# Seven adaLN blocks moved off TensorE: products on GpSimd, sums on ScalarE

## The chip, the cores and the metric

One core of a Trainium2 chip runs the whole program. The metric is device time in microseconds (us): the median of several executions. TensorE multiplies matrices, VectorE and ScalarE do elementwise work, GpSimd does elementwise work and issues DMAs, and SyncE issues most DMAs. Each engine works through its own list of instructions in a fixed order; semaphores let one engine wait for another.

## The reference

Two layers of a diffusion trunk for 128 context tokens and 256 sample tokens, D = 2048, all in float32. In each layer, for both token groups g (context with c_ctx, sample with c):

```
m = silu(cond) @ w_mod + b_mod            # 2048 -> 6144: shift, scale, gate
h = rms_norm(x, g) * (1 + scale) + shift
x = x + gate * mixer(h)                   # mixer: h @ w_in, branches, @ w_out
```

Layer 0's mixer has a convolution of 31 taps with a layer norm on one branch, and attention with normalized q and k on the other. Layer 1's has windowed attention and a gated convolution of three taps. A final RMS norm gives the outputs. What the change touches is the first line, `silu(cond) @ w_mod`: a product of two vectors with a 2048 x 6144 matrix, twelve blocks of 512 output columns per layer.

## The kernel before

**Tokens and weights.** All 384 tokens are held at once, x transposed by features (`xT`, 128 partitions x 16 chunks x 384). Each float32 product is made of three faster ones: a weight tile `raw` of 128x1024 is split by ScalarE into a rounded part `whi` (L261) and by VectorE into the rest `wlo` (L262), and h likewise into `hhi` and `hlo`. A unit of weights by features (`feat_unit`, L354) is two such tiles, with 24 matmuls of 384 columns for each. So TensorE needs, for every 24 matmuls, one cast of ScalarE and one subtraction of VectorE. Weight tiles come on SyncE's queue through `NRAW` = 7 buffers.

**adaLN.** Three ways are used. (1) `mod_part` with `gemv_block` (L139): the vectors c_ctx and c, after SiLU, are 32 columns of stationary weights and the 512-column blocks of w_mod stream through TensorE, 16 matmuls for a block; four transposes (L172) bring the result from rows to partitions; `mod_finish` adds the bias. (2) `mod_vector` (L197): VectorE multiplies and adds, loads on GpSimd's queue; used for layer 1's shift and gate. (3) Layer 0's scale and shift, needed first, are made by way (1) at the start.

**Stages.** At the start come the q projection with layer 0's scale (`q_unit`, L571) and the key/value projection with its shift (L333). Then follow layer 0's projections by features: the convolution's inputs for four pairs of chunks, with 31 taps for each of 8 chunks on VectorE (`conv_steps`, L659, 240 steps of 399 columns) and attention (`attention0`) after the second pair; the layer norm (`ln_mean`, `ln_center`, `ln_out`), whose sums run on GpSimd (L702, L704, L718); and two groups of gate projections (L735, L528). Then the output projection adds to `xT` with `mods[0, 2]` as the gate (L543), and near its end `make_h(1, k)` needs `mods[1, 1]`. Layer 1 and the final norm follow.

**What sets the order.** A scheduler places instructions by priority. Background adaLN steps wait in `gemv_q`; after each unit of weights `pump` takes `bg["rate"]` of them. In layer 0 the queue holds the bias of q (`bias_q`, 8 steps), layer 0's gate (4 blocks) and three of the four blocks of layer 1's scale, 4 steps for each block. Taps and `mod_vector` steps are put `LATER` and fill VectorE's gaps. Each engine then runs its list in order.

Of the kernel before, what the change touches and what calls it, by code (L numbers as in the profile page):

```python
# [19 lines left out]
P = 128  # L20
# [18 lines left out]
NRAW = 7  # L39
# [3 lines left out]
R0 = 1.7  # L43
# [8 lines left out]
def trunk(ctx: ExitStack, tc: tile.TileContext, d: dict, o: dict):  # L52
# [128 lines left out]

    def mod_vector(layer, part, j, av, ring):
# [60 lines left out]
    xT = big.tile([P, KC, T], F32, tag="bigA", name="xT")  # L243

    def square_sum():
        av = tmp.tile([P, T], F32, tag="sacc", name="sacc", bufs=1)

        def each(f):
            if f == 0:
                nc.scalar.activation(av, xT[:, f, :], AF.Square)  # L250
            else:
                s = tmp.tile([P, T], F32, tag="wk", bufs=4, name="sqf")
                nc.scalar.activation(s, xT[:, f, :], AF.Square)  # L253
                nc.gpsimd.tensor_tensor(av, av, s, ALU.add)  # L254
        return av, each
# [8 lines left out]
    def make_h(layer, k):  # L264
        for g, c0, c1 in GROUPS:
            a = mods[layer, 1][:, k, g:g + 1]
            nc.scalar.activation(hhi[:, k, c0:c1], xT[:, k, c0:c1], AF.Copy, scale=a)  # L267
            nc.vector.scalar_tensor_tensor(hlo[:, k, c0:c1], xT[:, k, c0:c1], a, hhi[:, k, c0:c1].bitcast(F32),
                                           ALU.mult, ALU.subtract)

    def scale_norm(layer, dst, k, rb):
        for g, c0, c1 in GROUPS:
            ins = nc.vector.scalar_tensor_tensor(dst[:, c0:c1], xT[:, k, c0:c1], mods[layer, 1][:, k, g:g + 1],
                                                 rb[:, c0:c1], ALU.mult, ALU.mult).ins
            tc.add_manual_dep(ins, order["split"].name, NOSYNC, reason="weights first")
# [258 lines left out]
    def out_proj(layer, w, mix, units, each, split_last=0, between=None):  # L534
# [4 lines left out]
        def ev(fb):  # L539
            def go(j, ps):  # L540
                f = 2 * fb + j
                for g, c0, c1 in GROUPS:
                    nc.vector.scalar_tensor_tensor(xT[:, f, c0:c1], ps[:, c0:c1], gate[:, f, g:g + 1], xT[:, f, c0:c1],  # L543
                                                   ALU.mult, ALU.add)
                each(f)
            return go
# [32 lines left out]
    for j, nf in enumerate(widths):  # L579
        n = nf // P  # L580
        with first():
            for _ in range(2048 // (2048 // nf * P)):
                scale_q.pop(0)()
            sync_load(xT[:, k0:k0 + n, :], d["xT"][:, k0:k0 + n, :])
            for k in range(k0, k0 + n):
                make_h(0, k)
# [13 lines left out]
    load_tables()  # L600
    kT, v = qkv_state(0)
# [65 lines left out]
    gemv_q.extend(bias_q + mod_part(0, 2) + mod_part(1, 1, (512,) * 3))  # L667
# [63 lines left out]
    for fb in range(4):  # L731
# [4 lines left out]
        proj_feat(w0[8 + fb], ev_a)  # L736
    evb = gate_mul(mix, 8)
# [121 lines left out]
    def y_block(q, t, new=aux, after=True):  # L859
        py = new("y_ps")  # L860
        for i in range(4):
            ins = nc.tensor.transpose(py[:, i * P:(i + 1) * P], xT[:, 4 * q + i, t * P:(t + 1) * P], ident).ins  # L862
# [4 lines left out]
    def each(f):  # L867
# [4 lines left out]
        else:  # L872
            tail.append(tmp.tile([P, T], F32, tag="wk", bufs=4, name="sqf"))
            nc.scalar.activation(tail[-1], xT[:, f, :], AF.Square)
        nc.vector.tensor_scalar(xT[:, f, :], xT[:, f, :], vcol("final_norm_g", f), None, ALU.mult)
# [45 lines left out]
def _layout(inputs):  # L921
    a = {name: np.asarray(x) for name, x in inputs.items()}
    out = {name: a[name] for name in _AS_IS}
    out["vecs"] = np.concatenate([a[name].reshape(n, P).T for name, n in _VECS], axis=1)
    out["xT"] = _by_rows(np.concatenate([a["x_prompt"][0], a["x_sample"][0]]))
# [48 lines left out]
```

## Time and profile before

| | us |
|---|---|
| median of 3 runs (1297.65 to 1298.38) | 1298.0 |
| span of the profiled execution (the time that the profile has for it) | 1295.9 |
| TensorE busy, share of the span | 1267.4, 98% |
| VectorE busy, share | 882.0, 68% |
| ScalarE busy, share | 544.5, 42% |
| GpSimd busy, share | 142.2, 11% |

The profile shows one execution. Its page has the busy time of each engine, the same in 40 slices of the span, the chain of work that ended last, and groups of instructions by source line. Further views cut the span into windows, list one engine's groups or instructions in a window, and follow the chain there. In them PE is TensorE, DVE is VectorE, ACT is ScalarE, POOL is GpSimd and SP is SyncE. The durations of neighbouring instructions can overlap, above all on PE; the time that one adds is read from a run of them.

### The profile page before, as it was taken

The numbers are of one execution on the slowest core, as the hardware profiler recorded it, in microseconds if no ns is written. First come the engines' busy times: TensorE is split into PE (matmuls) and PEld (weight loads), VectorE is DVE, ScalarE is ACT, GpSimd is POOL, SyncE is SP. The second block draws the span as 40 slices with busy tenths as digits, with TensorE's granted clock in tenths as the row PEclk, the third lists the DMA queues.
The fourth block names the chain that finished last, engine by engine and source line by source line (L and its number), as shares of the span: only waits on it lengthen the run. The fifth ranks groups of instructions, "written<-read, shape, count | busy, mean of one in ns | idle before, by whom it ended". The sixth has DMA issues, their size and how long they took to land.

```text
span 1295.9 us, 18150 instructions
## 1 busy us (share of the span) xinstructions
PE 1267.4 (98%) x7000; PEld 1123.1 (87%) x7000; DVE 882.0 (68%) x1464; ACT 544.5 (42%) x941; POOL 142.2 (11%) x162
## 2 busy tenths in 40 slices
PE   6999999999999999999999999999999999999997
PEld 4566687888887888999999988899999999999997
DVE  2245627899999979989976932454544689996443
ACT  3344433644556645432363633344444422343332
POOL 0210100210000042122220000000000011111110
PEclk9999999999999999999999999999999999999998
DMA  9988867688654566676644444433333577764412
GB/s 364 403 309 313 300 185 258 232 307 295 226 166 160 196 221 218 209 225 217 199 135 130 121 128 130 123 118 109 98 99 103 185 231 229 252 194 146 123 50 98
DMA packets 71222, 252.76 MB, mean 195 GB/s; under 512 B 7456, under 2 KB 11808, under 8 KB 67552
## 3 DMA queue, kind: packets, MB, share of 16 engines
q1 hardware_dynamic: 59920, 211.90, 48.9%
q0 software_dynamic: 11072, 39.60, 9.8%
q8 instruction: 55, 0.90, 0.3%
q14 instruction: 31, 0.25, 0.1%
q10 hardware_dynamic: 144, 0.10, 0.0%
HBM read 247.91 MB, written 3.67 MB: 194 GB/s over the span
## 4 chain that ended last, share of the span: by engine, by line
PE 85%; DMA 5%; DVE 5%; issue 3%; POOL 1%; ACT 1%; SPq 0%; DVEq 0%; POOLq 0%; ACTq 0%
PE pf L354 57%; PE pt L333 10%; PE q L571 6%; PE gv L139 5%; DMA area<-in_mod_w 3%; DVE area L197 2%; PE s_ps L470 2%; PE o_ps L495 2%; DVE wlo L262 1%; DMA raw<-in_wf 1%; PE pT_ps L491 1%; DMA ring<-in_mod_w 1%; PE gv L172 1%; POOL lvar L718 1%; PE y_ps L862 1%
## 5 line engine op out<-in xcount | busy, mean ns | idle before, releaser
L354 PE MATMUL pf<-hhi,whi 128*128 128x384 f32 (+1 forms) x1664 | 569.2, 342 | 0.7 <-ACT whi L261 0.7
L354 PE MATMUL pf<-hlo,whi 128*128 128x384 f32 (+1 forms) x1664 | 569.7, 342 | 0.0
L354 PE MATMUL pf<-hhi,wlo 128*128 128x384 f32 (+1 forms) x1664 | 567.2, 343 | 1.7 <-DVE wlo L262 1.7
L262 DVE TENSOR_TENSOR wlo<-raw,whi 128x1024 fp32r<-128x1024 f32 x256 | 314.8, 1230 | 294.3 <-ACT whi L261 288.9
L261 ACT CAST whi<-raw 128x1024 fp32r<-128x1024 f32 x256 | 268.3, 1049 | 466.3 <-PE pf L354 242.5
L354 PEld LDWEIGHTS pf<-hhi,whi 128*128 128x128 f32 x1664 | 313.1, 188 | 24.0 <-issue 14.2
L354 PEld LDWEIGHTS pf<-hhi,wlo 128*128 128x128 f32 x1664 | 313.3, 188 | 9.8 <-issue 3.2
L354 PEld LDWEIGHTS pf<-hlo,whi 128*128 128x128 f32 x1664 | 313.6, 188 | 5.3 <-issue 2.9
L197 DVE SCALAR_TENSOR_TENSOR area<-area,cst 128x512 f32<-128x512 f32 x240 | 177.8, 777 | 14.7 <-DMA area<-in_mod_w 14.5
L659 DVE SCALAR_TENSOR_TENSOR cv<-apad,cw,cv 128x399 f32<-128x399 f32 x240 | 140.6, 635 | 1.1 <-ACT cv L657 0.8
L91 POOL DMA_DIRECT2D area<-in_mod_w x64 | 34.7, 542 | 424.0 <-DVE area L197 222.0
L333 PE MATMUL pt<-wlo,hhi 128*128 128x512 f32 x192 | 75.8, 395 | 0.0
L254 POOL TENSOR_TENSOR sacc<-sacc,sqf 128x384 f32<-128x384 f32 x43 | 55.2, 1284 | 186.9 <-ACT sqf L253 185.1
L333 PE MATMUL pt<-whi,hhi 128*128 128x512 f32 x192 | 75.7, 397 | 0.0
L333 PE MATMUL pt<-whi,hlo 128*128 128x512 f32 x192 | 75.0, 396 | 0.0
L333 PEld LDWEIGHTS pt<-whi,hhi 128*128 128x128 f32 x192 | 36.0, 188 | 12.4 <-ACT hhi L280 2.5
L571 PE MATMUL q<-whi,hhi 128*128 128x512 f32 x96 | 41.1, 428 | 4.4 <-ACT hhi L267 4.4
L478 ACT ACTIVATE pr<-s_ps,nm 128x384 f32<-128x384 f32 (+1 forms) x48 | 24.4, 509 | 49.7 <-DVE nm L477 34.7
L333 PEld LDWEIGHTS pt<-whi,hlo 128*128 128x128 f32 x192 | 36.0, 188 | 10.1 <-issue 0.8
L333 PEld LDWEIGHTS pt<-wlo,hhi 128*128 128x128 f32 x192 | 36.1, 188 | 9.0 <-issue 0.8
L139 PE MATMUL gv<-ring,cst 128*32 128x512 f32 (+1 forms) x288 | 35.8, 582 | 8.2 <-DMA ring<-in_mod_w 7.6
L571 PE MATMUL q<-wlo,hhi 128*128 128x512 f32 x96 | 40.5, 422 | 0.0
(171 smaller groups left out, 991.8 us busy)
## 6 DMA issues: line engine op xcount, KB each, us to landing
raw<-in_wf SPq DMA_DIRECT2D x144, 512.0 KB, 4.5
ring<-in_mod_w SPq DMA_DIRECT2D x32, 1024.0 KB, 7.5
area<-in_mod_w POOLq DMA_DIRECT2D x64, 512.0 KB, 4.6
raw<-in_w_out SPq DMA_DIRECT2D x64, 512.0 KB, 4.4
raw<-in_mod_w SPq DMA_DIRECT2D x56, 512.0 KB, 5.6
raw<-in_wq SPq DMA_DIRECT2D x32, 512.0 KB, 8.8
raw<-in_wt SPq DMA_DIRECT2D x24, 512.0 KB, 3.6
raw<-in_wkv SPq DMA_DIRECT2D x8, 512.0 KB, 7.8
```

What stands on the lines that cost most here:

```text
L91: ins = nc.gpsimd.dma_start(dst, src).ins
L139: nc.tensor.matmul(ps[32 * g:32 * g + 32, :nf], lhsT=stat(k), rhs=raw[:, i % raw.shape[1], :], start=(k < 4), stop=(k >= KC - 4))
L197: nc.vector.scalar_tensor_tensor(av[:, g], raw[:, i], cst[:, 2 * k + g:2 * k + g + 1], av[:, g], ALU.mult, ALU.add)
L254: nc.gpsimd.tensor_tensor(av, av, s, ALU.add)
L261: nc.scalar.copy(dst_hi, src)
L262: order["split"] = nc.vector.tensor_tensor(dst_lo, src, dst_hi.bitcast(F32), ALU.subtract).ins
L333: nc.tensor.matmul(pp[t], lhsT=x[:, k, tt], rhs=y[:, i, :], start=(k == 0 and n == 0), stop=(k == KC - 1 and n == 2))
L354: ins = nc.tensor.matmul(pp[j][:, :n], lhsT=x[:, i, fj], rhs=y[:, k, :n], start=(begin and k % 8 == 0 and m == 0), stop=(end and k % 8 == ...
L470: nc.tensor.matmul(ps, lhsT=mix[:, h0 + h, t * P:(t + 1) * P], rhs=kT[:, kv, c0:c0 + nk * P], start=True, stop=True)
L495: nc.tensor.matmul(po, lhsT=v[:, slots[j], kv * HD:(kv + 1) * HD], rhs=pT[:, j, :], start=(j == 0), stop=(j == nk - 1))
L571: nc.tensor.matmul(pq[b][t], lhsT=x[:, k, tt], rhs=y[:, 0, 512 * b:512 * b + 512], start=(k == 0 and n == 0), stop=(k == KC - 1 and n == 2))
L659: nc.vector.scalar_tensor_tensor(st["o"], apad[:, c, j:j + CVW], cw[:, c, j:j + 1], st["o"], ALU.mult, ALU.add)
```

## The change

The seven blocks that `gemv_q` held in layer 0 beside `bias_q` (layer 0's gate, four blocks, and three blocks of layer 1's scale) no longer go through TensorE. The weights of adaLN are laid out transposed in HBM as well (`modT`): a tile of 128x2048 has 128 output features as partitions and the 2048 inputs as columns. `load_crow` broadcasts c_ctx and c to all partitions and applies SiLU (`crow`, 128 x 2 x 2048). `mod_rows` then loads, for each block, four such tiles of 1 MB on GpSimd's queue; for each half tile and each of the two vectors GpSimd multiplies 1024 columns with `crow`, and ScalarE copies the product and accumulates its sum into `sm`. Seven blocks make 28 tiles, 112 products and 112 sums. `mod_finish` adds the two halves and the bias on VectorE.

The tiles and products take the room of `xT` (the tag bigA): after the key/value projection x is given up there, and after the last `done` it is loaded a second time, 3 MB on GpSimd's queue, as `xT2`, for the output projection. So `xT` becomes `x["T"]` all over the code. Further, `NRAW` falls from 7 to 6, `R0`, the rate of background steps at the start of layer 0, rises from 1.7 to 2.0, and the scratch for DMA descriptors is set to 2048.

```diff
-NRAW = 7
+NRAW = 6
-R0 = 1.7
+R0 = 2.0
...
+    crow = const.tile([P, 2, D], F32, name="crow")
+
+    def load_crow():
+        for g, name in enumerate(("c_ctx", "c")):
+            side_load(crow[:, g, :], d[f"row_{name}"].rearrange("(a f) -> a f", a=1).broadcast_to([P, D]))
+        for g in range(2):
+            nc.scalar.activation(crow[:, g, :], crow[:, g, :], AF.Silu)
+
+    def mod_rows(layer, part, j, slots):
+
+        if (layer, part) not in mods:
+            mod_tile(layer, part)
+        raws, prods = slots
+        sm = const.tile([P, 4, 2, 2], F32, name=f"sm{layer}{part}{j}")
+        with later(LATER):
+            for i in range(4):
+                n = row_n["raw"]
+                row_n["raw"] += 1
+                raw = raws[n % len(raws)]
+                side_load(raw, d[f"modT{layer}"][16 * part + 4 * j + i])
+                for h in range(2):
+                    w = raw[:, h * 1024:(h + 1) * 1024]
+                    for g in range(2):
+                        if g == 0:
+                            row_n["prod"] += 1
+                            pr = prods[row_n["prod"] % len(prods)]
+                        else:
+                            pr = w
+                        nc.gpsimd.tensor_tensor(pr, w, crow[:, g, h * 1024:(h + 1) * 1024], ALU.mult)
+                        nc.scalar.activation(pr, pr, AF.Copy, accum_out=sm[:, i, g, h:h + 1])
+
+        def done():
+            mod_finish(layer, part, slice(4 * j, 4 * j + 4), sm)
+        return done
...
     load_tables()
+    load_crow()
...
-    gemv_q.extend(bias_q + mod_part(0, 2) + mod_part(1, 1, (512,) * 3))
+    gemv_q.extend(bias_q)
+    room = big.tile([P, KC * T], F32, tag="bigA", name="rows")
+    slots = ([room[:, :2048], room[:, 2048:4096]], [room[:, 4096:5120], room[:, 5120:6144]])
+    rows = [mod_rows(0, 2, j, slots) for j in range(4)] + [mod_rows(1, 1, j, slots) for j in range(3)]
...
         proj_feat(w0[8 + fb], ev_a)
+    for done in rows:
+        done()
+    x["T"] = big.tile([P, KC, T], F32, tag="bigA", name="xT2")
+    side_load(x["T"], d["xT"])
     evb = gate_mul(mix, 8)
...
+    for l in range(2):
+        out[f"modT{l}"] = a[f"mod_w{l}"].T.reshape(48, P, D)
...
-    nc = bacc.Bacc("TRN2", target_bir_lowering=False, num_devices=1)
+    nc = bacc.Bacc("TRN2", target_bir_lowering=False, num_devices=1, dynamic_dma_scratch_size=2048)
```

**Where instructions move.** First, GpSimd's list in layer 0 around the norm of q and k. `ss` is the mean square of each head (L434 before, L472 in the changed code), then its power of -1/2 (L214, L252); `out_new_k` stores the context's keys. Before:

```order
L91 DMA out_new_v<-v 128x256
L434 TENSOR_SCALAR ss<-ss 128x10
L214 TENSOR_TENSOR ss<-ss,mhalf 128x10
L434 TENSOR_SCALAR ss<-ss 128x10
L214 TENSOR_TENSOR ss<-ss,mhalf 128x10
L91 DMA out_new_k<-nat_772 128x256
```

In the changed program (a stretch of the same place), where `rows` are the tiles and products and `crow` the broadcast vectors:

```order
L91 DMA rows<-in_modT 128x2048
L211 TENSOR_TENSOR rows<-rows,crow 128x1024 x6
L91 DMA rows<-in_modT 128x2048
L211 TENSOR_TENSOR rows<-rows,crow 128x1024 x2
L91 DMA rows<-in_modT 128x2048
L211 TENSOR_TENSOR rows<-rows,crow 128x1024 x6
L472 TENSOR_SCALAR ss<-ss 128x10
L211 TENSOR_TENSOR rows<-rows,crow 128x1024
L472 TENSOR_SCALAR ss<-ss 128x10
L91 DMA rows<-in_modT 128x2048
L211 TENSOR_TENSOR rows<-rows,crow 128x1024
L252 TENSOR_TENSOR ss<-ss,mhalf 128x10 x2
```

GpSimd had only the norm's small steps and loads to do there; now the norm's steps stand between products, and a load of a tile stands behind the product and the sum that free its room.

Second, GpSimd's list at the layer norm: `lsum` is the sum over chunks of the convolution's output, `lvar` that of the squares. Before:

```order
L702 TENSOR_TENSOR lsum<-apad 128x384
L91 DMA mix_1213<-in_mod_w 128x1024 x6
L704 TENSOR_TENSOR lsum<-lsum,apad 128x384 x6
L91 DMA area<-in_mod_w 128x1024 x4
L718 TENSOR_TENSOR lvar<-lvar,sql 128x384 x6
L91 DMA area<-in_mod_w 128x1024
L718 TENSOR_TENSOR lvar<-lvar,sql 128x384
```

In the changed program, near the end of the products:

```order
L211 TENSOR_TENSOR rows<-rows,crow 128x1024
L746 TENSOR_TENSOR lsum<-lsum,apad 128x384
L211 TENSOR_TENSOR rows<-rows,crow 128x1024
L91 DMA area<-in_mod_w 128x1024
L746 TENSOR_TENSOR lsum<-lsum,apad 128x384
L211 TENSOR_TENSOR rows<-rows,crow 128x1024 x2
L91 DMA area<-in_mod_w 128x1024
L91 DMA rows<-in_modT 128x2048
L211 TENSOR_TENSOR rows<-rows,crow 128x1024 x2
L760 TENSOR_TENSOR lvar<-lvar,sql 128x384
L91 DMA area<-in_mod_w 128x1024 x2
L211 TENSOR_TENSOR rows<-rows,crow 128x1024 x2
```

The adds of the layer norm, which followed each other with loads between, now have one or two products between them; the last products stand after the first of `lvar`.

Third, ScalarE's list in layer 0's attention, for the first context head group: `pr` are the probabilities, `pT` their transposes, `mix` takes the result, and `sgb` is a sigmoid of a projection. Before:

```order
L261 CAST whi<-raw 128x1024
L478 ACT_TABLE_LOAD
L478 ACTIVATE pr,den<-s_ps,nm 128x128
L261 CAST whi<-raw 128x1024
L478 ACTIVATE pr,den<-s_ps,nm 128x128
L486 ACTIVATE pr<-pr,den 128x128 x4
L261 CAST whi<-raw 128x1024
L492 COPY pT<-pT_ps 128x512
L261 CAST whi<-raw 128x1024
L497 COPY mix_1213<-o_ps 128x4x128
```

In the changed program:

```order
L299 CAST whi<-raw 128x1024
L715 ACT_TABLE_LOAD
L715 ACTIVATE sgb<-pf_2979 128x384
L212 ACTIVATE rows,sm_1314<-rows 128x1024
L524 ACTIVATE pr<-pr,den 128x128 x4
L299 CAST whi<-raw 128x1024
L212 ACTIVATE rows,sm_1314<-rows 128x1024
L530 COPY pT<-pT_ps 128x512
L299 CAST whi<-raw 128x1024
L212 ACTIVATE rows,sm_1314<-rows 128x1024
L212 ACTIVATE rows,sm_1351<-rows 128x1024
L535 COPY mix_1218<-o_ps 128x4x128
```

Between the casts of the weights now stand the sums of the products (L212), each of which waits for GpSimd.

## Rows read from the trace of the kernel before

**Rows 1.** The page: engines' busy time, and slices of the span in tenths.

```profile
PE 1267.4 (98%) x7000; PEld 1123.1 (87%) x7000; DVE 882.0 (68%) x1464; ACT 544.5 (42%) x941; POOL 142.2 (11%) x162
...
DVE  2245627899999979989976932454544689996443
...
PEclk9999999999999999999999999999999999999998
```

**Rows 2.** Windows: stretch, then busy us and count of each engine, as headed.

```profile
core 0: us, PE busy (x) PEld busy (x) DVE busy (x) ACT busy (x) POOL busy (x), PEclk, DMA share, GB/s
165.00:511.00 346.00, 341.08 (x1940) 284.78 (x1938) 292.50 (x481) 179.85 (x349) 40.85 (x41) 1.00 0.67 223
165.00:275.00 110.00, 108.21 (x631) 89.15 (x632) 74.36 (x118) 51.86 (x139) 11.26 (x11) 1.00 0.71 234
...
400.00:511.00 111.00, 107.87 (x593) 90.29 (x592) 98.65 (x160) 64.22 (x99) 22.17 (x21) 1.00 0.59 193
```

**Rows 3.** TensorE's groups, 165 to 511: busy us, mean ns | idle before.

```profile
L139 PE MATMUL gv<-raw,cst 128*32 128x512 f32 x224 | 33.8, 603 | 0.0
...
L172 PE MATMUL gv<-ident,gs 128*128 128x128 f32 x28 | 4.2, 273 | 0.0
```

**Rows 4.** The chain in order of time: start us, us, what.

```profile
181.41 1.85 PE gv L139 x16
...
484.83 0.49 PE gv L172 x4
```

**Rows 5.** VectorE's groups, 165 to 511: columns as in rows 3.

```profile
L659 DVE SCALAR_TENSOR_TENSOR cv<-apad,cw,cv 128x399 f32<-128x399 f32 x240 | 140.6, 635 | 1.1 <-ACT cv L657 0.8
L262 DVE TENSOR_TENSOR wlo<-raw,whi 128x1024 fp32r<-128x1024 f32 x59 | 73.6, 1248 | 47.9 <-ACT whi L261 47.5
...
L197 DVE SCALAR_TENSOR_TENSOR mix<-mix,cst 128x512 f32<-128x512 f32 x30 | 21.4, 738 | 0.0
L475 DVE TENSOR_REDUCE nm<-s_ps 128x1 f32<-128x384 f32 (+1 forms) x24 | 11.0, 459 | 3.2 <-PE s_ps L470 3.0
```

**Rows 6.** GpSimd's instructions, 74 to 84 and 470 to 484: start, us.

```profile
76.48 4.83 POOL L254 TENSOR_TENSOR sacc<-sacc,sqf 128x384 f32<-128x384 f32 x4 [17.38 <-ACT sqf L253]
...
471.31 10.69 POOL L718 TENSOR_TENSOR lvar<-lvar,sql 128x384 f32<-128x384 f32 x6 [0.76 <-ACT sql L717]
```

**Rows 7.** VectorE's instructions, 470 to 484 us.

```profile
469.64 3.83 DVE L711 TENSOR_TENSOR apad<-apad,mean 128x384 f32<-128x384 f32 x8
...
476.25 2.04 DVE L262 TENSOR_TENSOR wlo<-raw,whi 128x1024 fp32r<-128x1024 f32 x1
478.21 2.92 DVE L197 SCALAR_TENSOR_TENSOR area<-area,cst 128x512 f32<-128x512 f32 x2
```

**Rows 8.** VectorE's instructions, 396 to 400 us.

```profile
397.90 2.47 DVE L659 SCALAR_TENSOR_TENSOR cv<-apad,cw,cv 128x399 f32<-128x399 f32 x3
```

**Rows 9.** GpSimd's instructions, 396 to 400 us.

```profile
397.55 1.30 POOL L704 TENSOR_TENSOR lsum<-lsum,apad 128x384 f32<-128x384 f32 x1 [39.39 <-ACT apad L663]
```

**Rows 10.** ScalarE's groups, 165 to 511 us.

```profile
L261 ACT CAST whi<-raw 128x1024 fp32r<-128x1024 f32 x60 | 62.8, 1048 | 100.1 <-DMA raw<-in_wf 71.4 <-PE pf L354 25.5 <-ACT pr L478 1.5
...
L433 ACT ACTIVATION_READ_ACCUMULATOR mix<-nat 128x1 f32 x30 | 5.7, 190 | 0.0
```

**Rows 11.** The page: DMA issues, count, KB each, median us to landing.

```profile
ring<-in_mod_w SPq DMA_DIRECT2D x32, 1024.0 KB, 7.5
...
raw<-in_mod_w SPq DMA_DIRECT2D x56, 512.0 KB, 5.6
```

**Rows 12.** The chain in order of time, 448 to 516 us.

```profile
456.22 1.43 POOL lsum L704
...
498.70 3.83 DVE apad L721 x8
...
511.26 4.85 PE pf L354 x26
```

**Rows 13.** Line 543: count, ns min/median/max, first and last start.

```profile
L543 DVE SCALAR_TENSOR_TENSOR xT<-pf,mod,xT x64: 341/412/478, 543.8 to 1280.2; 128x128 f32<-128x128 f32 x32, 128x256 f32<-128x256 f32 x32
```

More of the change, by code (lines that the diff above doesn't have):

```diff
@@ L180, in mod_part @@
         return units
+    crow = const.tile([P, 2, D], F32, name="crow")
[28 more added lines that the diff above has]
+        return done
+    row_n = {"raw": 0, "prod": 0}
     def mod_vector(layer, part, j, av, ring):
@@ L241, in rstd_rows @@
         return rb
-    xT = big.tile([P, KC, T], F32, tag="bigA", name="xT")
+    x = {"T": big.tile([P, KC, T], F32, tag="bigA", name="xT")}
     def square_sum():
@@ L249, in each @@
             if f == 0:
-                nc.scalar.activation(av, xT[:, f, :], AF.Square)
+                nc.scalar.activation(av, x["T"][:, f, :], AF.Square)
             else:
                 s = tmp.tile([P, T], F32, tag="wk", bufs=4, name="sqf")
-                nc.scalar.activation(s, xT[:, f, :], AF.Square)
+                nc.scalar.activation(s, x["T"][:, f, :], AF.Square)
                 nc.gpsimd.tensor_tensor(av, av, s, ALU.add)
@@ L272, in scale_norm @@
         for g, c0, c1 in GROUPS:
-            ins = nc.vector.scalar_tensor_tensor(dst[:, c0:c1], xT[:, k, c0:c1], mods[layer, 1][:, k, g:g + 1],
+            ins = nc.vector.scalar_tensor_tensor(dst[:, c0:c1], x["T"][:, k, c0:c1], mods[layer, 1][:, k, g:g + 1],
                                                  rb[:, c0:c1], ALU.mult, ALU.mult).ins
@@ L583, in trunk @@
                 scale_q.pop(0)()
-            sync_load(xT[:, k0:k0 + n, :], d["xT"][:, k0:k0 + n, :])
+            sync_load(x["T"][:, k0:k0 + n, :], d["xT"][:, k0:k0 + n, :])
             for k in range(k0, k0 + n):
@@ L873, in each @@
             tail.append(tmp.tile([P, T], F32, tag="wk", bufs=4, name="sqf"))
-            nc.scalar.activation(tail[-1], xT[:, f, :], AF.Square)
-        nc.vector.tensor_scalar(xT[:, f, :], xT[:, f, :], vcol("final_norm_g", f), None, ALU.mult)
+            nc.scalar.activation(tail[-1], x["T"][:, f, :], AF.Square)
+        nc.vector.tensor_scalar(x["T"][:, f, :], x["T"][:, f, :], vcol("final_norm_g", f), None, ALU.mult)
         if f % 4 == 1 and f > 4:
@@ L924, in _layout @@
     out["vecs"] = np.concatenate([a[name].reshape(n, P).T for name, n in _VECS], axis=1)
+    for name in ("c_ctx", "c"):
+        out[f"row_{name}"] = a[name].reshape(-1)
+    for l in range(2):
+        out[f"modT{l}"] = a[f"mod_w{l}"].T.reshape(48, P, D)
     out["xT"] = _by_rows(np.concatenate([a["x_prompt"][0], a["x_sample"][0]]))
```

8 lines of the change are left out of this document (4 added, 4 removed).

## The prediction

> **What bounds the kernel now.** I read the page first. TensorE is busy for 98% of the span and the granted clock is full nearly throughout, so the whole kernel looks bound by TensorE; but the slices of VectorE stand at 9 for long stretches in the first half [rows 1]. So I cut the span by stages. The change works between the end of the key/value projection and the start of layer 0's output projection, 165 to 511 us. There TensorE is busy for 341.1 of 346 us, VectorE for 292.5, ScalarE for 179.9 and GpSimd for 40.9 [rows 2]. VectorE has 53.5 us idle in all of it, most of it early: 35.6 of them before 275 us, 12.4 after 400. In this stage two engines are nearly full, and the third and fourth have room. The work taken away is TensorE's, the work added is GpSimd's and ScalarE's; the question is what the added work does to VectorE, the other full engine, which makes the low half of every weight tile (wlo) that TensorE waits for.
>
> **What is removed.** Seven blocks of 16 narrow matmuls and four transposes each. The trace has two records for each of these matmuls: 224 records, and 28 transposes, all inside the stage [rows 3]. Their mean durations overlap, so I price them by the chain, where 16 records take 1.85 us and 4 transposes 0.49 us [rows 4]: 14 x 1.85 + 7 x 0.49 = 25.9 + 3.4 = 29.3 us of TensorE. That is all that can be won, and only while TensorE stays the bound. Seven evictions on ScalarE go too, and 56 loads of 512 KB on SyncE's queue [rows 11].
>
> **What is added on ScalarE.** 112 sums over 1024 columns. Nothing like it is in the trace; a cast of 1024 columns takes 1.05 us and reading an accumulator 0.19 us [rows 10], so 112 x 1.24 = 139 us. ScalarE then has 180 + 139 = 319 us in a stage of 346 us or more: it fits, if it is not held up. But each sum waits for its product on GpSimd, and the casts that make whi stand behind the sums in ScalarE's order; a late product delays the weights.
>
> **What is added on GpSimd, and what it takes from VectorE.** 112 products of 128x1024, read from two SBUF tiles. The nearest rows are adds of 128x384. Four of them in a row take 4.83 us [rows 6]; one of the four began beside a wlo, and taking off some 0.6 us for that leaves 1.05 us each, an estimate. From 471 to 484 us the trace shows adds side by side with VectorE. Two of VectorE's 512-column steps then take 2.92 us, 1.46 each [rows 7], where the same step alone takes 0.74 [rows 5]; a wlo takes 2.04 [rows 7] where the mean of the stage is 1.25 [rows 5]; and three convolution taps beside one add take 2.47 us [rows 8, 9] where three alone need 3 x 0.59 = 1.76 (140.6 us busy over 240, [rows 5]). So each add of 384 columns holds VectorE up by 0.71 to 0.8 us, three quarters of the add's own time. They do not share; they take turns.
>
> [...]
>
> For a product of 1024 columns the hold is unknown. From below: it does not grow with the columns, 0.72 us. From above: it is a whole add scaled by its columns, 1.05 x 1024 / 384 = 2.8 us. I take the hold scaled by its columns, 0.77 x 2.67 = 2.05 us, since the work that holds the port is the reading of the columns. 112 x 2.05 = 230 us.
>
> What of this is hidden? Taps and wlo, 214 us of VectorE's 292.5, and most of the rest have two SBUF inputs; the reductions of the scores (11.0 us) and under 20 us of other PSUM reads can run beside a product [rows 5]. VectorE's idle time of 53.5 us can hide products only where one is ready while VectorE waits, and 47.9 us of it is waiting for whi from ScalarE [rows 5], which the sums now delay. I let half of the idle time hide, 27 us. So VectorE's stage grows by 230 - 27 = 203 us. TensorE's 29.3 us then buy nothing: it waits for wlo instead. After the stage the order of the work is as before, and the rest of the span is shifted.
>
> **Edits that I cost at nothing.** Reloading x, 3 MB from GpSimd's queue behind the last product: 1 MB lands in 7.5 us [rows 11], so about 22 us; its first use is an eviction at 543.8 [rows 13], 32 us after the output projection starts. If the last product comes later than that start, up to 22 us stand free. The 28 loads of 1 MB carry the same bytes as the 56 removed, at a DMA share of 0.67 [rows 2]; the two broadcasts of the conditioning rows, 2 MB, land under the key/value projection. One weight buffer less (7 to 6) is covered by the loads that leave the same queue. The layer norm's adds on GpSimd now stand between products: the norm's chain ran from its last sum at 456 to the first scaled block at 499 us [rows 12], beside projections. If TensorE has run out of those by then, up to 42 us stand free; I take 0, because VectorE is already counted as full there.
>
> **Sum.** The profiled execution's span is 1295.9 us, and the median of the runs is 1298.0, 2.1 us more. 1295.9 + 203 = 1498.9, with the 2.1: 1501, which I round to 1500 us.
>
> **Rivals.**
> *VectorE keeps the port* (15%). For it: from 469.6 eight subtractions with two SBUF inputs ran in 3.83 us without loss [rows 7], while the adds beside them waited (six adds took 10.69 us, [rows 6]). Against it: taps and wlo did lose. Then GpSimd gets only what VectorE leaves, and the stage is long enough for both: about 265 us of two-input work plus 230 is 495, 149 over the 346. 1298 + 149 = 1447.
> *The whole instruction excludes* (12%). The hold would be 1.05 x 2.67 = 2.8 us; 112 x 2.8 - 27 = 287: 1585 us.
> *GpSimd's queue is the bound, not the port* (8%). If the hold does not grow with the columns, VectorE loses 112 x 0.72 = 81 us, of which idle time and PSUM work take most. Products of 2.8 us make 314 us, with GpSimd's own 41 us 355, against 346 - 29 = 317: 38 us late. The layer norm's adds stand in that queue, so its chain of 42 us comes behind them uncovered; with TensorE's 29 us won: 1298 - 29 + 38 + 42 = 1349.
> [...]
> *It does what it says* (4%): faster. Place: VectorE's idle time and its PSUM reads. If products ran only there, or in turns with no loss, and GpSimd's 355 us fitted beside the layer norm, TensorE's 29.3 us would be won: 1298 - 29 = 1269. It decides from a hold per product below 53.5 / 112 = 0.48 us, less than the 384-column add shows, so it needs a hold that shrinks with the columns.
>
> **How the numbers follow.** My sum has 60%, and its own range is 1465 to 1535 (all of the idle time hides, or none of it and 2.1 us per hold). The four rivals have 15, 12, 8 and 4%, and 1% is left for no change. The range takes in the first two rivals. Its low end also takes a hold of which 0.3 us is fixed: 0.3 + 0.42 x 2.67 = 1.42, 112 x 1.42 - 53.5 = 106, 1404; I set 1395. The high end is whole instructions, rounded up to 1590. Outside are the last two rivals and tails, some 15%. A measurement of this kernel tells 0.2% from no change, 2.6 us. Only the last rival is faster: 0.04; same 0.01; slower 0.95.
>
> **What would show it.** Right: in the changed profile, TensorE's busy share between the key/value projection and the output projection falls well under 98%, its waits name wlo, whi and through them VectorE; taps that took 0.63 us have a mean of 1.5 us or more, wlo one of 2 us or more; products take 2.3 to 4 us each; the output projection starts some 200 us later, and from there to the end the time is as before. The rival of VectorE's port: taps keep 0.63 us and products take longer than 4 us. Whole instructions: taps prolonged by 2.8 us each time. GpSimd's queue: taps and wlo nearly as before, and TensorE stands only at the layer norm's matmuls or at the output projection's first evictions. The forecast is wrong if wlo and taps keep their means, or if the time after the output projection's start changes by more than some 20 us.

## The result, and the profile after

The changed kernel takes 1511.0 us (median of four runs, 1510.64 to 1511.38) against 1298.2 us for the kernel before: a ratio of 1.163, 95% interval 1.161 to 1.165, or 213 us more. The forecast was 1500.

The page of the changed kernel answers to [rows 1]: first the busy time of each engine, then slices of the span in tenths, then two of its groups (busy us, mean ns of one | idle time before, and its releaser).

```profile
PE 1283.4 (85%) x6748; PEld 1155.1 (77%) x6748; DVE 1111.0 (74%) x1464; ACT 655.2 (43%) x1158; POOL 443.7 (29%) x305
...
PE   7999878577768577322999999999999999999997
...
DVE  2345739999999999998998958624554368999443
...
PEclk9999989888888889655999999999999999999999
...
L392 PE MATMUL pf<-hhi,wlo 128*128 128x384 f32 (+1 forms) x1664 | 583.5, 354 | 91.6 <-DVE wlo L300 91.6
...
L211 POOL TENSOR_TENSOR rows<-rows,crow 128x1024 f32<-128x1024 f32 x112 | 287.0, 2585 | 36.8 <-ACT rows L212 35.6
```

VectorE has as many instructions as before, 1464, and is busy 229 us longer. Its nines now run on where TensorE's have gone. The lines have shifted: the taps are line 698 (before 659), wlo line 300 (262), VectorE's own steps on area and mix line 235 (197); the products themselves are line 211, the sums line 212.

Where does the stage end? The prediction took 511 us for the start of the output projection, from a piece of the chain in [rows 12]. That piece lies in the last group of gate projections, whose two results ScalarE takes up only at 526 and 529 us (the first of the two, before and in the changed kernel, stands below). In the changed kernel they are taken up at 740 and 743 us:

```profile
526.29 0.49 ACT L528 ACTIVATE sg<-pf 128x384 f32<-128x384 f32 x1 [1.44 <-PE pf L354]
...
739.97 0.49 ACT L566 ACTIVATE sg<-pf 128x384 f32<-128x384 f32 x1 [1.46 <-PE pf L392]
```

Counted by matmuls, the output projection starts at 527.5 us before (after 1536 matmuls by features) and at 740.8 us in the changed kernel, 213 us later. The windows by stage, columns as in [rows 2], first of before, from there and to the end, then of the changed kernel; one shows 58 us inside the stage's end:

```profile
165.00:527.50 362.50, 357.32 (x2032) 301.02 (x2031) 309.00 (x508) 189.79 (x367) 44.00 (x43) 1.00 0.68 224
527.50:1295.90 768.40, 759.04 (x4193) 726.00 (x4192) 501.41 (x792) 287.09 (x449) 71.35 (x88) 1.00 0.48 151
```

```profile
165.00:740.80 575.80, 375.71 (x1786) 334.55 (x1786) 540.45 (x528) 296.80 (x581) 338.74 (x182) 0.81 0.43 145
165.00:275.00 110.00, 89.15 (x455) 75.89 (x455) 82.31 (x75) 63.30 (x144) 70.92 (x38) 0.89 0.59 207
275.00:640.00 365.00, 246.20 (x1145) 223.49 (x1143) 364.43 (x341) 186.28 (x351) 221.59 (x108) 0.83 0.38 126
656.00:714.00 58.00, 6.77 (x21) 5.57 (x22) 51.05 (x52) 16.08 (x30) 33.46 (x27) 0.50 0.41 145
740.80:1509.50 768.70, 758.72 (x4194) 725.94 (x4192) 498.56 (x786) 287.11 (x450) 69.94 (x86) 1.00 0.47 151
```

The stage took 362.5 us and takes 575.8: 213.3 more. What follows takes 768.7 us, against 768.4 before. So the whole loss is in the one stage. From 275 to 640 us VectorE is busy for 364.4 of 365 us and TensorE for 67% of them: VectorE is the bound there. The granted clock, 1.00 throughout the stage before, is 0.81 here, and 0.50 from 656 to 714 us, where TensorE is busy for 6.77 of 58 us. Its busy time in the stage grows from 357 to 376 us although it has less to do. Where VectorE is full, from 275 to 640 us, TensorE at 0.83 still stands for 119 of the 365 us; what the lower clock costs in the rest of the stage no run shows.

VectorE's groups from 165 to 735 us, to be set against [rows 5]:

```profile
L698 DVE SCALAR_TENSOR_TENSOR cv<-apad,cw,cv 128x399 f32<-128x399 f32 x240 | 279.5, 1204 | 0.5
L300 DVE TENSOR_TENSOR wlo<-raw,whi 128x1024 fp32r<-128x1024 f32 x63 | 92.7, 1474 | 11.3 <-ACT whi L299 11.3
...
L235 DVE SCALAR_TENSOR_TENSOR mix<-mix,cst 128x512 f32<-128x512 f32 x30 | 47.2, 1600 | 0.0
```

The same 240 taps cost 139 us more, the same 30 steps of mix 26 us more. Setting every VectorE instruction between 140 and 740 us against the median of its shape in the trace of before, 89 are longer by over 0.25 us, 237 us in all, and 234 us of it lie in instructions beside a product: 2.09 us for each of the 112 products. But the median tap is still 0.62 us. The loss lies in few long instructions, as VectorE's timeline (start, us, what) shows:

```profile
256.79 1.72 DVE L698 SCALAR_TENSOR_TENSOR cv<-apad,cw,cv 128x399 f32<-128x399 f32 x3
...
259.56 9.75 DVE L698 SCALAR_TENSOR_TENSOR cv<-apad,cw,cv 128x399 f32<-128x399 f32 x4
...
273.48 13.60 DVE L698 SCALAR_TENSOR_TENSOR cv<-apad,cw,cv 128x399 f32<-128x399 f32 x2
```

Beside it GpSimd's timeline of the same stretches:

```profile
260.09 7.16 POOL L211 TENSOR_TENSOR rows<-rows,crow 128x1024 f32<-128x1024 f32 x3
273.85 0.60 POOL L91 DMA_DIRECT2D out_new_k<-nat  x1 [6.60 <-DVE nat L479]
274.48 6.99 POOL L211 TENSOR_TENSOR rows<-rows,crow 128x1024 f32<-128x1024 f32 x3
281.39 0.58 POOL L91 DMA_DIRECT2D rows<-in_modT  x1
281.99 4.64 POOL L211 TENSOR_TENSOR rows<-rows,crow 128x1024 f32<-128x1024 f32 x2
```

Three taps with no product beside them take 1.72 us. The four taps from 259.56 take 9.75 while three products run one behind the other. The two from 273.48 take 13.60: VectorE gets past only when GpSimd has finished five products in a row, with a DMA issue between them. But such rows of products are the exception. Of the 84 VectorE instructions that lose over 0.25 us beside a product, 60 lose 1.4 to 2.3 us, about one product, which takes 2.33 us at least; five lose less, 19 more. In the next lines, VectorE's and then GpSimd's, the engines take turns:

```profile
442.42 2.75 DVE L698 SCALAR_TENSOR_TENSOR cv<-apad,cw,cv 128x399 f32<-128x399 f32 x1
445.10 3.54 DVE L235 SCALAR_TENSOR_TENSOR mix<-mix,cst 128x512 f32<-128x512 f32 x2
```

```profile
441.18 6.26 POOL L211 TENSOR_TENSOR rows<-rows,crow 128x1024 f32<-128x1024 f32 x2 [4.47 <-ACT rows L212]
```

A tap of 0.62 us takes 2.75 beside the first product, a step of 0.74 stands for the second, and the two products take 6.26 us in place of 4.7, because they wait as well. Only seven products, between 197 and 226 us, prolong nothing: VectorE waits for most of that time. The other 105 cost VectorE 2.23 us each. While GpSimd waits for a sum or a load, VectorE runs many taps at 0.62 us each.

TensorE's waits in the changed kernel (total us, times, longest):

```profile
PE pf L392 <- DVE wlo L300: 91.6, 17, 15.0
PE rsl L258 <- POOL lvar L760: 47.2, 1, 47.2
```

And the chain at the end of the stage, answering to [rows 12]:

```profile
655.66 7.88 DVE area L235 x4
...
666.23 4.64 POOL rows L211 x2
...
680.89 8.44 DVE area L235 x3
...
706.19 1.01 POOL lvar L760
707.25 1.45 PE rsl L258 x6
...
732.99 47.09 PE pf L392 x267
```

TensorE first waits for wlo all through the stage, then once for 47.2 us at the layer norm, whose chain passes through VectorE steps that are held themselves (three steps of area take 8.44 us) and through additions that stand behind products. The last line begins in the last gate group and runs on into the output projection, whose first eviction follows:

```profile
L581 DVE SCALAR_TENSOR_TENSOR xT<-pf,mod,xT x64: 337/412/479, 759.4 to 1494.0; 128x128 f32<-128x128 f32 x32, 128x256 f32<-128x256 f32 x32
```

### The profile page after: what moved, and what is told of

It is laid out like the page before. It is cut to its first block, busy times and chain, and to the rows that moved or that the text cites. A ratio compares the mean times of both kernels' runs of the same rounds, so it can differ in the third digit from the quotient of the medians.

```text
span 1509.5 us, 17963 instructions
## 1 busy us (share of the span) xinstructions
PE 1283.4 (85%) x6748; PEld 1155.1 (77%) x6748; DVE 1111.0 (74%) x1464; ACT 655.2 (43%) x1158; POOL 443.7 (29%) x305
## 3 DMA queue, kind: packets, MB, share of 16 engines
q1 hardware_dynamic: 51856, 182.54, 35.4%
## 4 chain that ended last, share of the span: by engine, by line
PE 61%; DVE 28%; issue 6%; DMA 3%; POOL 1%; ACT 1%; SPq 0%; DVEq 0%; POOLq 0%; ACTq 0%
PE pf L392 41%; DVE cv L698 15%; PE pt L371 9%; PE q L609 5%; DVE wlo L300 5%; DVE area L235 3%; DVE mix L235 2%; PE gv L139 2%; DMA area<-in_mod_w 1%; PE o_ps L533 1%; PE s_ps L508 1%; DMA raw<-in_wf 1%; DVE mix L435 1%; DMA ring<-in_mod_w 1%; DVE nm L513 0%
## 5 line engine op out<-in xcount | busy, mean ns | idle before, releaser
L392 PE MATMUL pf<-hhi,wlo 128*128 128x384 f32 (+1 forms) x1664 | 583.5, 354 | 91.6 <-DVE wlo L300 91.6
L300 DVE TENSOR_TENSOR wlo<-raw,whi 128x1024 fp32r<-128x1024 f32 x256 | 330.9, 1294 | 254.6 <-ACT whi L299 250.1
L211 POOL TENSOR_TENSOR rows<-rows,crow 128x1024 f32<-128x1024 f32 x112 | 287.0, 2585 | 36.8 <-ACT rows L212 35.6
L698 DVE SCALAR_TENSOR_TENSOR cv<-apad,cw,cv 128x399 f32<-128x399 f32 x240 | 279.5, 1204 | 0.5
L235 DVE SCALAR_TENSOR_TENSOR area<-area,cst 128x512 f32<-128x512 f32 x240 | 195.2, 853 | 17.6 <-DMA area<-in_mod_w 17.3
L212 ACT ACTIVATE rows<-rows 128x1024 f32<-128x1024 f32 x112 | 118.0, 1054 | 31.5 <-POOL rows L211 31.4
L508 PE MATMUL s_ps<-kT,mix 128*128 128x384 f32 (+1 forms) x96 | 35.3, 452 | 22.5 <-ACT pr L516 22.3
L235 DVE SCALAR_TENSOR_TENSOR mix<-mix,cst 128x512 f32<-128x512 f32 x30 | 47.2, 1600 | 0.0
L91 POOL DMA_DIRECT2D rows<-in_modT x28 | 16.3, 584 | 104.8 <-ACT rows L212 54.0
L529 PE MATMUL pT_ps<-ident,pr 128*128 128x128 f32 x112 | 25.6, 326 | 22.6 <-ACT pr L524 21.8
```

The costliest lines, as they stand in the source:

```text
L91: ins = nc.gpsimd.dma_start(dst, src).ins
L211: nc.gpsimd.tensor_tensor(pr, w, crow[:, g, h * 1024:(h + 1) * 1024], ALU.mult)
L212: nc.scalar.activation(pr, pr, AF.Copy, accum_out=sm[:, i, g, h:h + 1])
L235: nc.vector.scalar_tensor_tensor(av[:, g], raw[:, i], cst[:, 2 * k + g:2 * k + g + 1], av[:, g], ALU.mult, ALU.add)
L300: order["split"] = nc.vector.tensor_tensor(dst_lo, src, dst_hi.bitcast(F32), ALU.subtract).ins
L392: ins = nc.tensor.matmul(pp[j][:, :n], lhsT=x[:, i, fj], rhs=y[:, k, :n], start=(begin and k % 8 == 0 and m == 0), stop=(end and k % 8 == ...
```

## The experiments

The theory: a product on GpSimd keeps VectorE out, and VectorE's time is what the stage lacks. The chief rival: GpSimd's queue (or ScalarE's, or one of the other edits) is what comes late. All edits are made in the changed kernel.

**Without the products.** The sums read the weight tile itself.

```
-    nc.gpsimd.tensor_tensor(pr, w, crow[...], ALU.mult)
-    nc.scalar.activation(pr, pr, AF.Copy, accum_out=...)
+    nc.scalar.activation(pr, w, AF.Copy, accum_out=...)
```

> The changed kernel without the 112 products on GpSimd: ScalarE sums the weight tiles as they are, so the adaLN vectors of the seven blocks are wrong; loads, sums, the second load of x and all sizes stay. Theory of the port (each product shuts VectorE out of its second SBUF input for some 2.1 us, 237 us in all): VectorE gets the 237 us back and TensorE keeps the 29 us, 1511 - 237 = 1274, within 1265 to 1300; taps never over 0.7 us. Theory of the sums (ScalarE's 139 us, with the casts queued behind them, and the loads are the cost): 1400 or more.

Measured: 1319.2 us, ratio 1.0165 (1.0135 to 1.0194), above the first expectation's 1300 and far under the second's 1400. The products are worth 191.9 of the 213 us. But 21 us are left above before, and the 29 us of TensorE's work that went are not won: some 50 us that I had not counted. The windows of this kernel, the whole stage and two stretches, then the two stretches of before:

```profile
165.00:547.20 382.20, 340.25 (x1791) 306.14 (x1790) 308.15 (x519) 291.89 (x576) 58.67 (x70) 0.94 0.63 216
...
275.00:330.00 55.00, 54.70 (x319) 54.44 (x318) 48.97 (x82) 54.44 (x105) 10.24 (x16) 1.00 0.85 305
330.00:400.00 70.00, 67.19 (x372) 63.17 (x371) 53.72 (x93) 68.67 (x123) 7.00 (x11) 1.00 0.68 234
```

```profile
275.00:330.00 55.00, 55.00 (x338) 47.26 (x332) 53.02 (x92) 26.37 (x48) 3.90 (x7) 1.00 0.85 294
330.00:400.00 70.00, 70.00 (x385) 58.09 (x385) 66.48 (x114) 37.40 (x65) 3.52 (x3) 1.00 0.61 198
```

In the two stretches ScalarE is full, 123.1 of 125 us against 63.8, since with no product to wait for the sums come one upon the other; VectorE, which waits for ScalarE's casts, is busy 17 us less there. In the whole stage VectorE is as busy as before (308 us) and idle for 74.0 us, against 53.5 before and 35.4 in the change.

**GpSimd as busy, but reading nothing.** Each product becomes three fills of 1024 columns.

```
-    nc.gpsimd.tensor_tensor(pr, w, crow[...], ALU.mult)
+    for _ in range(3):
+        nc.gpsimd.memset(pr, 1.0)
```

> Each product is replaced by three GpSimd memsets of 1024 columns, so that GpSimd is busy about as long (some 2.6 us per product) and in the same places of the waits, but reads nothing; the sums are of constants, the seven blocks wrong. Theory of the port: a write without reads leaves VectorE alone; GpSimd is only late, 1270 to 1350. Theory of GpSimd's queue (sums, the norm of q and k and the layer norm wait behind a busy GpSimd): about as slow as the change, 1450 to 1520.

Measured: 1332.6 us, ratio 1.0268 (1.0199 to 1.0338), inside the first expectation: 13 us over the kernel without products, not 192. Its taps, against a mean of 1204 ns in the changed kernel, and its fills:

```profile
L699 DVE SCALAR_TENSOR_TENSOR cv<-apad,cw,cv 128x399 f32<-128x399 f32 x240 | 142.6, 637 | 1.3 <-ACT cv L697 1.2
```

```profile
L212 POOL MEMSET rows<- 128x1024 f32 x336 | 307.0, 963 | 20.1 <-ACT rows L213 11.5 <-DMA rows<-in_modT 7.8 <-DVE hlo L320 0.2
```

GpSimd is busy for 307 us, longer than with the products (287), and the taps don't notice (637 ns, 635 before). TensorE waits once for 42.1 us at the layer norm, whose additions stand between fills, so a busy queue is not free; but the kernel is 178 us faster than the change. That GpSimd is occupied cost little here, 13 us; with products, which read SBUF, it cost 192.

**Half the columns.** Products and sums over 512 of the 1024 columns.

```
-    nc.gpsimd.tensor_tensor(pr, w, crow[...], ALU.mult)
-    nc.scalar.activation(pr, pr, AF.Copy, accum_out=...)
+    nc.gpsimd.tensor_tensor(pr[:, :512], w[:, :512], crow[:, g, h * 1024:h * 1024 + 512], ALU.mult)
+    nc.scalar.activation(pr[:, :512], pr[:, :512], AF.Copy, accum_out=...)
```

> 112 products and sums, each over 512 of its 1024 columns (half of every product of vector and weight is left out, so the seven blocks are wrong). Hold in proportion to the columns: half of 237 us goes, 1511 - 118 = 1393, 1370 to 1415, and a stalled tap is prolonged by about 1.1 us per product instead of 2.1. Hold per instruction: as the change, 1490 to 1515.

Measured: 1373.3 us, ratio 1.0582 (1.0552 to 1.0613), inside the first expectation. By the same count as above, VectorE's instructions beside products are 105 us longer, 0.94 us for each of 112 (2.09 with all columns). Here the hold grows with the columns, as my term took it.

**Each product in two halves.** 224 products of 512 columns, the same sums.

```
-    nc.gpsimd.tensor_tensor(pr, w, crow[...], ALU.mult)
+    for z in range(0, 1024, 512):
+        nc.gpsimd.tensor_tensor(pr[:, z:z + 512], w[:, z:z + 512],
+                                crow[:, g, h * 1024 + z:h * 1024 + z + 512], ALU.mult)
```

> Each product is split into two instructions of 512 columns, 224 in all, the same result. Theory of the port: the same columns hold VectorE for the same time, 1505 to 1540. Theory of bursts (the cost is that several products follow each other without letting VectorE in, up to 13 us, longer than TensorE's weight buffers last, not the total): VectorE gets in twice as often, stalls shorten, below 1470.

Measured: 1529.5 us, ratio 1.1786 (1.1751 to 1.182), 18 us slower than the change. The hold is 231 us, about as before (1.03 for each of 224), but spread over 144 VectorE instructions in place of 89. So more and shorter stalls save nothing, against the theory of bursts: the sum of the reading counts. GpSimd's own time grew, two products of 1.30 us (median) for one of 2.43. Of the 18 us, VectorE's busy time in the stage has 6 and its idle time 13; what it waits for there is not shown.

**One block.** One block of seven by rows, six on TensorE.

```
-    gemv_q.extend(bias_q)
+    gemv_q.extend(bias_q + mod_part(0, 2, (512,) * 3, 512) + mod_part(1, 1, (512,) * 3))
...
-    rows = [mod_rows(0, 2, j, slots) for j in range(4)] + [mod_rows(1, 1, j, slots) for j in range(3)]
+    rows = [mod_rows(0, 2, 0, slots)]
```

> One adaLN block of 512 columns goes by products and sums, the other six stay on TensorE as before; same result. Port theory (VectorE held 2.12 us per product, the first 25 to 50 us of it hidden in VectorE's idle time): 16 products hold 34 us, so 0 to 12 us remain, less 4 us of TensorE's work: 1295 to 1310. Rival, a fixed cost (the tile read twice, one raw buffer less, the layer norm late as soon as any product stands on GpSimd): 1315 or more, as in the kernel without products (1319).

Measured: 1336.6 us, ratio 1.0298 (1.027 to 1.0326). The first expectation missed: 39 us for 25 us of hold. The rival's "1315 or more" takes the time in, but its 1319 is 17 us too low. VectorE's and GpSimd's timelines of this kernel, and then a piece of its chain, show a part of why:

```profile
182.37 2.35 DVE L300 TENSOR_TENSOR wlo<-raw,whi 128x1024 fp32r<-128x1024 f32 x2
...
209.41 9.31 DVE L300 TENSOR_TENSOR wlo<-raw,whi 128x1024 fp32r<-128x1024 f32 x2 [3.00 <-ACT whi L299]
...
217.98 0.59 POOL L91 DMA_DIRECT2D xT<-in_xT  x1 [1.48 <-ACT rows L212]
```

```profile
209.41 8.19 DVE wlo L300
217.62 0.37 SPq L98
...
218.59 13.88 DMA raw<-in_wf
232.57 1.05 ACT whi L299
233.65 1.24 DVE wlo L300
```

The products stand at the stage's start. Two wlo that take 2.35 us alone take 9.31 beside them. In the chain SyncE issues the next load only once that wlo is done, and 13.88 us of DMA follow before TensorE has its next weights. A part of these belongs to this kernel alone: with one block the products end early, and the second load of x, 3 MB, is issued at 217.98 us, just ahead of those weights (in the change two loads at the same place, beside a tile of 1 MB, took 9.1 and 9.8 us). Most of the idle time of VectorE in which I hid a part of the products is early, where this loop of load, cast and wlo runs; here a hold in the loop was paid, and VectorE's idle time in the stage grew from 53.5 to 60.8 us instead of shrinking. How the 39 us divide between the hold, the loop and the load of x is not shown.

**Three blocks.** The same edit with three blocks of seven.

> Three blocks by products and sums, four on TensorE; same result. One block cost 39 us (1336.6) for 33 us of hold, seven cost 213. If the time goes in proportion to the products' hold (48 products x 2.12 = 102 us), with nothing hidden as in the kernel with one block: 1298 + 102 less 0 to 27 hidden = 1373 to 1405. Rival, a cost of starting (the first block stands in front of the stage's first casts, later products are partly hidden): 1350 to 1372.

Measured: 1380.9 us, ratio 1.0635 (1.0617 to 1.0653), inside the theory's range. 48 products hold VectorE for 89 us and cost 83. The steps are +39 for the first 16 products, +44 for the next 32 and, with the sums' and the layer norm's share, +130 for the last 64: 1.4 to 2.4 us for each. The cost grows with the products; a small cost of starting in the first 39 us is not excluded.

**VectorE does the products itself.** Product and sum in one instruction, nothing on GpSimd or ScalarE.

```
-    nc.gpsimd.tensor_tensor(pr, w, crow[...], ALU.mult)
-    nc.scalar.activation(pr, pr, AF.Copy, accum_out=...)
+    nc.vector.scalar_tensor_tensor(pr, w, 1.0, crow[...], ALU.mult, ALU.mult, accum_out=...)
```

> Product and sum of all seven blocks in one VectorE instruction each (two read operands, sum over the row), nothing on GpSimd or ScalarE; same result. If VectorE's time is the currency, 112 instructions of about 1.3 us (the 1024-column subtraction wlo takes 1.22) are 146 us in place of the 237 that GpSimd's products held: 1298 - 29 + 146 less about 27 to 50 hidden = 1365 to 1400, some 110 to 145 us faster than the change, though VectorE now does the arithmetic itself. Rival, the time of the change comes from GpSimd's and ScalarE's queues and not from VectorE: VectorE has 400 us idle in all, 1270 to 1320. Rival, a cost of the changed order whatever the engine: 1500.

Measured: 1438.7 us, ratio 1.1089 (1.1065 to 1.1113): 72 us faster than the change, though the fullest engine does all of the arithmetic. The 112 instructions take 1.217 us each (median), 136 us in all (145 with reading the sums out), and the time is 132.5 us above the kernel with neither products nor sums (below). So nearly all of VectorE's added time is paid; my 1365 to 1400 had hidden 27 to 50 us and won 29 that don't come. TensorE ran ahead of VectorE and then stood once, at the layer norm's first sum:

```profile
PE mean L748 <- POOL lsum L746: 118.6, 1, 118.6
```

**The other edits alone.** All seven blocks on TensorE as before; one raw buffer less, x loaded twice, the order's other constants; the conditioning rows are not loaded.

```
-    load_crow()
...
-    gemv_q.extend(bias_q)
...
-    rows = [mod_rows(0, 2, j, slots) for j in range(4)] + [mod_rows(1, 1, j, slots) for j in range(3)]
+    gemv_q.extend(bias_q + mod_part(0, 2) + mod_part(1, 1, (512,) * 3))
+    rows = []
```

> All seven blocks on TensorE as before, but with the rest of the change: one raw buffer less, the input x loaded twice, the other constants of the order; the row of the conditioning vector isn't loaded. Same result. If these edits cost nothing, as I took: 1293 to 1303. Rival (the x load or the buffer make the 50 us that the kernel without products is above 1269): 1320 to 1350.

Measured: 1301.5 us (ten runs), ratio 1.0027 (1.0014 to 1.0041): 3.7 us. Together these edits cost little, as I had taken. The rows that it leaves out are loaded in the next kernel, which is 4.7 us slower although TensorE has less to do.

**Neither products nor sums.** The loads stay; the sum covers 16 columns.

```
-    nc.gpsimd.tensor_tensor(pr, w, crow[...], ALU.mult)
-    nc.scalar.activation(pr, pr, AF.Copy, accum_out=...)
+    nc.scalar.activation(pr[:, :16], w[:, :16], AF.Copy, accum_out=...)
```

> Leaves out all products, and the sums but for 16 of each 1024 columns, so GpSimd has none of the seven blocks and ScalarE 112 short instructions in place of 118 us; the loads and everything else as in the change. If the 50 us by which the kernel without products stands above 1269 are ScalarE's (its 118 us of sums delay the casts behind them): 1269 to 1285. Rival (they are the loads', the second x load's or the missing buffer's): 1310 to 1320 as without products.

Measured: 1306.2 us, ratio 1.0062 (1.0041 to 1.0083), between the two expectations. ScalarE's sums are thus 13 us of the 50 (1319.2 - 1306.2), and 37 are left, 8 above before and the 29 not won. The rest is mostly neither of what I had set against each other: TensorE, with 29 us less to do, stands for 33.5 us at the layer norm, waiting for VectorE's taps and the steps behind them.

```profile
PE mean L747 <- POOL lsum L745: 19.1, 1, 19.1
PE rsl L257 <- POOL lvar L759: 14.4, 1, 14.4
```

**Products with one operand.** The tile times a constant.

```
-    nc.gpsimd.tensor_tensor(pr, w, crow[...], ALU.mult)
+    nc.gpsimd.tensor_scalar(pr, w, 0.5, None, ALU.mult)
```

> Each product reads one operand instead of two (the weight tile times a constant, so the conditioning vector is left out of the result): GpSimd still reads and writes 1024 columns, in one instruction as before. If VectorE is held by GpSimd reading at all: near 1440 to 1511, with single taps of 1.5 us and more. If it is the second read operand that holds it: 1319 to 1335, as without products or with writes alone, and no tap over 1.3 us.

Measured: 1424.3 us, ratio 1.0974 (1.0958 to 1.0991), a little below the range of the first expectation and its second half (single taps of 1.5 us) is off too: a tap beside such a product mostly takes 1.40 us in place of 0.62. The group of the taps and the products of this kernel (ns min/median/max, first and last start):

```profile
L698 DVE SCALAR_TENSOR_TENSOR cv<-apad,cw,cv 128x399 f32<-128x399 f32 x240 | 178.7, 788 | 0.3
```

```profile
L211 POOL TENSOR_SCALAR rows<-rows x112: 2760/2807/6342, 159.2 to 678.7; 128x1024 f32<-128x1024 f32 x112
```

These products are longer (2.81 us median against 2.43) but hold VectorE for less: by the count above 94 us beside products, 0.84 for each, in place of 2.09. Only a part of such a product stands in the way: of the 31 taps that begin in the first 1.2 us of one and end within it, 29 take over 1 us, and of the 62 that begin later 60 take 0.6. Yet the time falls by 87 us only, where the hold fell by some 140 (96 us of prolonged VectorE instructions in place of 237). TensorE hardly waits for wlo now (6.8 us), but once for lvar at the layer norm (61.6 us) and once for x at the output projection (37.9 us): something else has become the bound, which the next pair asks.

**The layer norm's additions on VectorE.** In the change, and in the kernel with one-operand products.

```
...
-    nc.gpsimd.tensor_tensor(av, av, apad[:, c, :T], ALU.add)
+    nc.vector.tensor_tensor(av, av, apad[:, c, :T], ALU.add)
...
-    nc.gpsimd.tensor_tensor(ln["v"], ln["v"], s, ALU.add)
+    nc.vector.tensor_tensor(ln["v"], ln["v"], s, ALU.add)
```

> The change with the layer norm's 15 additions (lsum, lvar) on VectorE instead of GpSimd, so that they no longer stand between products; same result. If VectorE's hold alone sets the time, TensorE's 47.2 us wait for lvar is only where the lateness shows: 1500 to 1520 (VectorE has 15 x 0.55 = 8 us more to do). Rival, the layer norm is late because its additions queue behind products: 1465 to 1490.

> The kernel with one-operand products (1424, the conditioning vector left out of them) with the layer norm's additions on VectorE. There VectorE was held only about 0.78 us per product (some 86 us in all) and TensorE waited 61.6 us for lvar, whose additions stood two products apart. If the queue before the layer norm was the rest: 1365 to 1400, near 1319 + 86 less what is hidden. Rival, the hold is the whole time there too: 1415 to 1430.

Measured: 1499.4 us, ratio 1.1541 (1.1524 to 1.1558), for the first, just under VectorE's range and above the rival's: 11.6 us off the change, against 47.2 us of waiting at the layer norm. So a quarter of that wait was worth time; the rest only showed how late VectorE was (the wait for lvar fell to 21.0 us, that for wlo rose from 91.6 to 107.6). For the second 1420.0, ratio 1.0934 (1.0914 to 1.0954): 4 us, the expected 1365 to 1400 missed. TensorE's waits say where it went:

```profile
PE pf L392 <- DVE xT L581: 83.7, 1, 83.7
```

TensorE now passes the layer norm, fills its accumulators and stands at the output projection's first evictions. These need x again; GpSimd issues its second load at 678.2 us, right behind the last sum, and the first eviction starts at 688.9. With VectorE held less, GpSimd's queue of products (the last starts at 674.0) is the next bound in this kernel, at about 1420 us.

## Why the prediction was right

The forecast was 1500, the time is 1511, and the step that carried it (a product keeps VectorE out in proportion to its columns) is shown by four runs: take the reading away and the taps are as before (fills), halve it and the hold halves, cut it in two and the total stays, let VectorE do the work and the time falls. In the sum's own terms, from 165 us to the true start of the output projection: VectorE's busy time grew by 231.5 us (I had 230) and its idle time shrank by 18.1 (I had 27), 213 together, where I had 203.

- *Hold per product, 2.05 us:* 2.09 measured, 0.94 for half the columns. Right in size, but by two errors that cancel, which is luck: I took three quarters of a product of 2.8 us, scaled from an addition; a product takes 2.33 us at least and 2.43 in the median, and nearly all of it is held, 2.23 us for each of the 105 products that held anything up. These 2.23 us are close to a whole product; my rows' three quarters were not. But the one-operand product held VectorE for 0.84 of its 2.81 us, so a hold for the whole instruction was not what every read of SBUF brought. That the reading of the columns holds a port was my assumption, and no run shows a port. The runs show the taps' mean, 635 ns before, at 1204 with two-operand products, 788 with one operand and 637 with fills, and the hold at 0.94 us for half the columns.
- *The engines take turns:* mostly so (60 of 84 held instructions stand for about one product), though up to five products passed in a row. The forecast of taps with a mean of 1.5 us or more and wlo of 2 us or more failed (1.20 and 1.47). The two together would have been some 250 us, more than the 230 of my own sum; and the hold fell not only on the taps (139 us of it) but also on the steps of line 235 (47).
- *Hidden, 27 us:* 18 against before. VectorE's reads of PSUM did run beside products: the 17 of them that overlapped one in the changed kernel (scores, `pf`, `gv`) took the median of before to within 0.02 us. Against the kernel without products the idle time shrinks by 39 us (74.0 to 35.4), which is the most of the 42 by which 234 us of hold exceed 191.9 of time. Of VectorE's early idle time, which I named as the place, some 8 us went (35.6 before 275 us, then 27.7), and the single block, which lies in it, cost 39 us for a hold of 25. The low end of the sum's own range was also added wrongly: 1298 + 230 - 53.5 is 1474, not 1465.
- *TensorE's 29.3 us buy nothing:* right. Without products and sums the kernel is 8 us slower than before, not 29 faster. The waiter there is other than named: with wlo on time, TensorE stands at the layer norm, behind VectorE's taps.
- *ScalarE fits:* the sums took 1.05 + 0.19 us as priced, but cost 13 us, taken at 0, in the kernel without products; what they cost in the change no run shows.
- *Edits costed at nothing:* 3.7 us for the buffer, the second x load and the order; the second load took some 10 us to the first eviction, not 22 (in the last kernel above), and in the change came early enough. The layer norm's additions, taken at 0 of up to 42, cost 11.6.
- *What would show it:* products of 2.3 to 4 us (2.59 mean), the output projection some 200 us later (213.3), the time behind it within 20 us (768.7 against 768.4), TensorE's waits naming wlo: all so. Its start I had read wrongly, 511 us for 527.5; the sum did not use it, but the room for reloading x is then 16 us, not 32.
- *Rivals:* "VectorE keeps the port" falls with the long taps and the products' 2.59 us; "the whole instruction excludes" (1585) charged 2.8 us, from an addition's time scaled by its columns, where a product takes 2.43; its whole instruction is nearer to the 2.23 us held than my sum's three quarters. "GpSimd's queue" was no bound here, by the fills (1333); with one-operand products it became one, at about 1420. Why it is so much later there than with fills, no run shows. "It does what it says" fails twice, by the hold and by the 29 us that nobody could use.

## What to carry to other kernels

Before moving work to GpSimd, ask which engine is second in that stage and whether the moved work reads SBUF: here 287 us of GpSimd took 234 us from VectorE, and the same arithmetic on VectorE itself took 136. Removing work from the busiest engine may win nothing: here TensorE was busy for 99% of the stage and VectorE for 85%, and the 29 us were not won. A run that removes the work and adds only the loads (1306 against 1298 here) shows that first. Idle time inside a loop of load, cast and use need not be room: the one block that lay there cost 39 us for a hold of 25. And before the end of a stage is read from a chain, count its matmuls or find its first use.

## What the runs showed of the hardware that was not expected

- GpSimd's products can pass one behind the other while a VectorE instruction stands: two taps took 13.60 us through five products and a DMA issue of GpSimd. In most cases the engines took turns, and a product waited in its turn (2.59 us in the mean, 2.33 at least). What decides between the two is open.
- A one-operand multiply of 128x1024 is slower on GpSimd than the two-operand one (2.81 against 2.43 us median), but holds VectorE for 0.84 us instead of 2.09, and taps mostly only where they begin in its first 1.2 us; beside fills of the same size (0.97 us) the taps are as before (637 ns against 635).
- While TensorE stood at the layer norm, from 656 to 714 us in the changed kernel, its granted clock was 0.50, and TensorE was busy for 6.77 of the 58 us; before, no slice of the span before its last was below 9 tenths.
